# Attention stage: transposes of the outputs into the projection's PSUM tile, one projection product per unit by a table of steps, the final norm shared by ScalarE and VectorE

## The chip, the core and the metric

The kernel runs on one core of a Trainium2 chip. The metric is device time in microseconds (us) of one execution; the figure to beat is the median of three runs. A profile of one execution gives each engine's instructions: PE is TensorE's matmuls (PEld its weight loads), DVE is VectorE, ACT is ScalarE, POOL is GpSimd, SP is SyncE, which here only issues transfers (a q behind a name, as in SPq, means the engine's instruction queue).

## The reference, cut to what matters

The model has two layers; the change is in the second one, an attention over 2304 keys (256 of a context, 2048 of the sequence) for 2048 queries, 16 query heads that share 4 key heads, and in what follows it:

```
def attention_mixer(...):
    ...
    o_l = blocked_attention(q_l, k_all, v_all)      # softmax(q k / 8) v, head by head
    out_l = (o_l * jax.nn.silu(g_l)) @ w_out        # 2048 x 1024 by 1024 x 1024
    ...
def reference(...):
    ...
        h_lat = h_lat + gate[:, None] * o_lat
    return rms_norm(h_lat) * final_gain
```

`rms_norm` divides each row by the root of its mean square.

## The kernel before

`odd_attention` is the last stage of the program. The 2048 queries lie in 16 query tiles of 128 rows. A **unit** `u` is one query tile with one head, so there are 256 units, and 16 in a row make a query tile (`u // 16`). A loop runs over units and, inside a unit, over `b` = 0, 1, 2 (three thirds of the keys, 768 each). It is a hand-written software pipeline: in loop `u` the program works on four units at once, in this order:

- `s_step(u + 2, b)`: scores on PE into one of two PSUM buffers `s`, from which DVE copies them to `st` and takes their running maximum `mx` (line 1998);
- `split_step(u)` at b = 1: ACT makes the f16 high half `hi` of the transposed probabilities; `pv_end(u - 1)` at b = 2: ACT copies the result `r`;
- `exp_step(u + 1, b)`: ACT's exponential of `st` (line 2006), which needs the maximum over all three thirds; `n_step(u + 1, b)` at b = 0, 1: POOL splits probabilities into f16 halves `nat`;
- `t_step(u)` at b = 0: eight PE transposes of probabilities into the PSUM tile `tp` (line 2025), which has one buffer;
- `pv_step(u - 1)` at b = 0 and 1: 36 PE products with the values into `pv`;
- `d_step(u + 1, b)`: SP issues the transfer that transposes `nat` into `T`;
- `lower_step(u)` at b = 1: DVE makes the low half `lo` from `tp` (line 2035);
- then one entry of `small` (POOL's three steps on the outputs `o`) and one entry of the queue `todo[b]`.

When loop `w` = 16 (qt + 1) has ended a query tile, `finish` fills `todo[1]` and `todo[2]` with that tile's projection, and one entry of the queue of that `b` is taken per unit. Counting loops from `w`, the queues do this:

- loops w+1 and w+2, b = 2: `tr(0)` and `tr(1)`, four PE transposes of `o` each, **into a `tp` tile**, and from it ACT's `oh` (line 2102) and DVE's `ol` (line 35). `tr(0)` also loads the residual rows `h`;
- loops w+3 to w+13: the 16 products `mm` (three matmuls of 512 columns each, lines 2111 to 2113), three in two loops. `mm` 7 and 15 end an accumulation in the PSUM tile `po` (one buffer), and DVE adds it to `h` (line 2115);
- loop w+13: `norm`, ACT's square with a sum and two small POOL steps; w+14 and w+15, b = 1: `end(0)` and `end(1)`, one DVE instruction each (line 2122); w+16: the store.

So of the 16 loops between one `w` and the next, w+14, w+15 and w+16 have no product, w+1 and w+2 have the transposes. PSUM has eight banks; `s` takes four, `tp` two, `pv` and `po` one each.

Of the kernel before, what the change touches and what calls it, by code (L numbers as in the profile page):

```python
# [9 lines left out]
F32 = mybir.dt.float32  # L10
# [3 lines left out]
AF = mybir.ActivationFunctionType  # L14
ALU = mybir.AluOpType
# [4 lines left out]
P = 128  # L20
DM = 1024
KC = DM // P
T = 2304
NCTX = 256
# [9 lines left out]
def sub_lo(eng, lo, full, hi):  # L34
    eng.tensor_tensor(out=lo, in0=full, in1=hi.bitcast(F32), op=ALU.subtract)  # L35
# [10 lines left out]
def rms_rstd(E, pool, x, width, tag, junk):  # L46

    nc = E.nc
    ss = pool.tile([P, 1], F32, tag=tag + "s", name=tag + "s")
    nc.scalar.activation(out=junk, in_=x, func=AF.Square, accum_out=ss)  # L50
    r = pool.tile([P, 1], F32, tag=tag + "r", name=tag + "r")
    nc.gpsimd.tensor_scalar(out=r, in0=ss, scalar1=1.0 / width, scalar2=EPS, op0=ALU.mult, op1=ALU.add)
    nc.gpsimd.tensor_tensor(out=r, in0=r, in1=E.mhalf, op=ALU.pow)
    return r
# [1809 lines left out]
TCH = 8  # L1864
# [36 lines left out]
def odd_attention(E, out):  # L1901
    nc, I, S, tc = E.nc, E.I, E.S, E.tc
    v, gp = nc.vector, nc.gpsimd
    with ExitStack() as ctx:
        kp = ctx.enter_context(tc.tile_pool(name="at_k", bufs=2, side="right", reuse_waits="tile"))
        sp = ctx.enter_context(tc.tile_pool(name="at_l", bufs=2, reuse_waits="tile"))
# [3 lines left out]
        sps = ctx.enter_context(tc.tile_pool(name="at_s", bufs=1, space=PSUM, reuse_waits="tile"))  # L1910
        tps = ctx.enter_context(tc.tile_pool(name="at_t", bufs=1, space=PSUM, reuse_waits="tile"))
# [18 lines left out]
        fg = sp.tile([P, DM], F32, tag="fg", name="fg", bufs=1)  # L1930
# [44 lines left out]

        QT = [None] * 16
        UN = {}
        todo, small = ([], [], []), []

        def unit(u):  # L1980
            return u // 16, (u // 4) % 4, u % 4
# [22 lines left out]
        def exp_step(u, b):  # L2004
            st = UN[u]["st"][b]
            nc.scalar.activation(out=st, in_=st, func=AF.Exp, bias=UN[u]["mx"][:, 6:7])  # L2006
# [9 lines left out]
        def d_step(u, b):  # L2016
            T = UN[u]["T", b] = pp.tile([P, 2 * DCH[b], P], F16, tag=f"T{b}", name="T", bufs=2)
            nc.sync.dma_start_transpose(out=T, in_=UN[u]["nat", b].rearrange("p a c -> p (a c)"))
# [8 lines left out]
        def split_step(u):  # L2027
            hi, lo = [pp.tile([P, TCH, P], F16, tag=n, name=n, bufs=2) for n in ("hi", "lo")]
            pt = UN[u]["pt"]
            nc.scalar.activation(out=hi, in_=pt, func=AF.Copy)  # L2030
            UN[u]["hl"] = hi, lo
# [26 lines left out]
        def pv_end(u):  # L2058
            qt, kv, hh = unit(u)
            pv = UN[u]["pv"]  # L2060
            if u % 16 == 3:
                QT[qt] = sp.tile([P, DM], F32, tag="o", name="o", bufs=1)
            if u % 16 == 0:
                SG[qt] = sp.tile([P, DM], F32, tag="sg", name="sg", bufs=1)
                nc.sync.dma_start(out=SG[qt], in_=S["sg"][qt * P:(qt + 1) * P, :])
            if hh == 0:
                QR[kv % 2] = sp.tile([P, 4, 130], F32, tag="r", name="r")
            R = QR[kv % 2]
            nc.scalar.activation(out=R[:, hh, 0:129], in_=pv[:, 0:129], func=AF.Copy)
            if hh == 3:  # L2070
                oc = QT[qt][:, kv * 256:(kv + 1) * 256].rearrange("p (h d) -> p h d", d=HD)
                rs = sp.tile([P, 4, 1], F32, tag="rs", name="rs")
                v.reciprocal(rs, R[:, :, 64:65])
                of = QT[qt][:, kv * 256:(kv + 1) * 256]
                sgk = SG[qt][:, kv * 256:(kv + 1) * 256]
                small.extend([
                    lambda: gp.tensor_tensor(out=oc, in0=R[:, :, 0:64], in1=R[:, :, 65:129], op=ALU.add),
                    lambda: gp.tensor_tensor(out=oc, in0=oc, in1=rs.to_broadcast([P, 4, HD]), op=ALU.mult),
                    lambda: gp.tensor_tensor(out=of, in0=of, in1=sgk, op=ALU.mult)])
            del UN[u]  # L2080
            if u % 16 == 15:
                finish(qt)

        def finish(qt):

            qc = slice(qt * P, (qt + 1) * P)
            o = QT[qt]
            F = {}

            def tr(q):  # L2090
                if q == 0:
                    F["h"] = sp.tile([P, DM], F32, tag="h", name="h", bufs=1)
                    nc.sync.dma_start(out=F["h"], in_=S["h"][NCTX + qt * P:NCTX + (qt + 1) * P, :])
                    F["oh"] = sp.tile([P, KC, P], F32R, tag="oh", name="oh", bufs=1)
                    F["ol"] = sp.tile([P, KC, P], F32R, tag="ol", name="ol", bufs=1)
                pt = tps.tile([P, TCH, P], F32, tag="tp", name="tp")[:, :4].rearrange("p k t -> p (k t)")
                for k in range(4):
                    kk = 4 * q + k
                    nc.tensor.transpose(pt[:, k * P:(k + 1) * P], o[:, kk * P:(kk + 1) * P], E.ident)
                ks = slice(4 * q, 4 * q + 4)  # L2100
                p4 = pt.rearrange("p (k t) -> p k t", t=P)
                nc.scalar.activation(out=F["oh"][:, ks], in_=p4, func=AF.Copy)
                sub_lo(v, F["ol"][:, ks], p4, F["oh"][:, ks])

            def mm(c, k):
                cs = slice(c * 512, (c + 1) * 512)
                if k == 0:
                    F["po"] = sps.tile([P, 512], F32, tag="po", name="po", bufs=1)
                po, oh, ol = F["po"], F["oh"], F["ol"]
                wh, wl = W["wh"][:, k, cs], W["wl"][:, k, cs]  # L2110
                nc.tensor.matmul(po, oh[:, k], wh, start=(k == 0), stop=False)  # L2111
                nc.tensor.matmul(po, oh[:, k], wl, start=False, stop=False)  # L2112
                nc.tensor.matmul(po, ol[:, k], wh, start=False, stop=(k == KC - 1))  # L2113
                if k == KC - 1:
                    v.tensor_tensor(out=F["h"][:, cs], in0=po, in1=F["h"][:, cs], op=ALU.add)

            def norm():
                F["r"] = rms_rstd(E, sp, F["h"].rearrange("p (k c) -> p k c", c=P), DM, "fr", F["oh"])

            def end(c):  # L2120
                h, cs = F["h"], slice(c * 512, (c + 1) * 512)
                v.scalar_tensor_tensor(out=h[:, cs], in0=h[:, cs], scalar=F["r"], in1=fg[:, cs], op0=ALU.mult, op1=ALU.mult)

            def store():
                nc.sync.dma_start(out=out[qc, :], in_=F["h"])

            none = lambda: None
            products = [lambda c=c, k=k: mm(c, k) for c in range(2) for k in range(KC)]
            first = [none] * 2
            second = [none, lambda: tr(0), lambda: tr(1)]  # L2130
            while products:
                first.append(products.pop(0) if len(first) % 2 == 0 else none)
                if products:
                    second.append(products.pop(0))
            todo[1].extend(first + [lambda: end(0), lambda: end(1), store])
            todo[2].extend(second + [norm])

        NU = 256
        load_keys(0)
# [6 lines left out]
        for i in range(-2 * NTH, (NU + 2) * NTH):  # L2146
            u, b = divmod(i, NTH)
            if 0 <= i + VSTEP < NS // 3:
                values(i + VSTEP)
            out_weights(u, b)  # L2150
            live = lambda w: 0 <= w < NU
            if live(u + 2):
                s_step(u + 2, b)
            if b == 1 and live(u):
                split_step(u)
            if b == 2 and live(u - 1):
                pv_end(u - 1)
            if live(u + 1):
                exp_step(u + 1, b)
                if b < NTH - 1:  # L2160
                    n_step(u + 1, b)
            if b == 0 and live(u):
                t_step(u)
            if live(u - 1):
                for g in ((0,), (1, 2), ())[b]:
                    pv_step(u - 1, g)
            if live(u + 1) and b < NTH - 1:
                d_step(u + 1, b)
            if b == 1 and live(u):
                lower_step(u)  # L2170
            if small:
                small.pop(0)()
            if todo[b]:
                todo[b].pop(0)()
        while small:
            small.pop(0)()
        while todo[1] or todo[2]:
            for b in (1, 2):
                if todo[b]:
                    todo[b].pop(0)()  # L2180

# [151 lines left out]
```

## Time and profile before

| | |
|---|---|
| median of 3 runs | 4036.66 us (4035.59 to 4037.07) |
| profiled execution, its own time | 4034.8 us |
| its span, first to last instruction | 4033.1 us |
| attention loop in steady state | from about 2600 us to 4000 us |
| one query tile (16 units) in steady state | 92.19 us |

The profiled execution is 1.9 us below the median of the runs. A steady-state query tile repeats itself to within some hundredths of a us, so one of them, taken between the first probability transposes of loop w+1 (3182.16 us) and the same place 16 units later (3274.35 us), stands for all.

### The profile page before, as it was taken

How to read it: one execution, taken by the hardware profiler on the slowest of the kernel's cores; microseconds unless marked ns; L12 is line 12 of the kernel's file. 1: busy time of each engine (PE TensorE's matmuls, PEld its weight loads, DVE VectorE, ACT ScalarE, POOL GpSimd, SP SyncE). 2: the span in 40 equal slices, each digit the busy share in tenths (PEclk: the TensorE clock that was granted, in tenths of full speed). 3: DMA queues.
4: the chain of work that ended last, by engine and by line, in shares of the span. 5: the costliest groups of instructions: out<-in, count | busy, mean ns of one | idle time of the engine just before them, and what ended most of it. 6: DMA issues, size and time to landing. Idle time of an engine off the chain costs nothing.

```text
span 4033.1 us, 72188 instructions
## 1 busy us (share of the span) xinstructions
PE 3720.1 (92%) x27102; PEld 3145.1 (78%) x27102; DVE 2754.4 (68%) x5006; ACT 1850.9 (46%) x3195; POOL 2196.0 (54%) x2120
## 2 busy tenths in 40 slices
PE   7999998638889999999999997899999999999998
PEld 4888886316888888788778886788888888888887
DVE  5366767997687888711455453877777777777775
ACT  4422224203435565411222222666666666666665
POOL 2111113731233999522333332988888888888886
PEclk9999999869999999999999998999999999999999
DMA  7512323324667667533332225889888888888885
GB/s 262 176 56 66 98 69 93 109 66 118 210 221 257 228 235 241 191 123 131 129 110 85 94 79 146 173 143 159 162 157 154 154 153 157 152 151 158 153 163 115
DMA packets 998591, 594.49 MB, mean 147 GB/s; under 512 B 711849, under 2 KB 908249, under 8 KB 996193
## 3 DMA queue, kind: packets, MB, share of 16 engines
q1 hardware_dynamic: 984112, 563.35, 56.2%
q10 hardware_dynamic: 14128, 26.51, 1.8%
q8 instruction: 214, 3.51, 0.3%
q14 instruction: 137, 1.11, 0.1%
HBM read 296.63 MB, written 125.32 MB: 105 GB/s over the span
## 4 chain that ended last, share of the span: by engine, by line
PE 48%; DVE 5%; POOL 3%; issue 1%; DMA 1%; ACT 1%; SPq 0%; DVEq 0%; POOLq 0%; ACTq 0%
PE s L1996 11%; PE mm L43 6%; PE mm L41 6%; PE mm L42 6%; PE tp L2025 5%; PE pv L2054 5%; PE pv L2056 3%; PE po L2111 2%; DVE st L1998 2%; PE po L2112 1%; PE po L2113 1%; POOL nat L2014 1%; DVE lo L2035 1%; POOL nat L2013 1%; DVE ol L35 1%
## 5 line engine op out<-in xcount | busy, mean ns | idle before, releaser
L2006 ACT ACTIVATE st<-st,mx 128x768 f32<-128x768 f32 x768 | 714.5, 930 | 355.5 <-DVE mx L2002 271.8
L2014 POOL TENSOR_TENSOR nat<-st,nat 128x768 f16<-128x768 f32 (+1 forms) x512 | 727.0, 1420 | 42.7
L1996 PE MATMUL s<-KS,q 128*128 128x512 f32 (+1 forms) x3072 | 693.7, 351 | 40.3 <-DVE mx L1998 39.8
L1998 DVE CUSTOM_DVE_ANT_0 st<-s,zero,mx 128x768 f32<-128x768 f32 x512 | 519.3, 1014 | 278.8 <-PE s L1996 203.6
L1996 PEld LDWEIGHTS s<-KS,q 128*128 128x128 f32 x3072 | 536.1, 190 | 136.8 <-DVE mx L1998 47.7
L2013 POOL TENSOR_SCALAR nat<-st 128x768 f16<-128x768 f32 (+1 forms) x512 | 387.6, 757 | 187.4 <-ACT st L2006 187.2
L2025 PE MATMUL tp<-ident,st 128*128 128x128 f32 x2048 | 280.9, 277 | 36.4 <-DVE ol L35 22.3
L2035 DVE TENSOR_TENSOR lo<-tp,hi 128x1024 f16<-128x1024 f32 x256 | 312.3, 1220 | 2.9 <-ACT hi L2030 2.9
L2054 PE MATMUL pv<-V,T 128*128 128x129 f16 x2560 | 310.8, 222 | 2.4 <-DMA T<-nat 2.3
L41 PE MATMUL mmps<-ah,wh 128*128 128x512 f32 (+1 forms) x800 | 304.7, 381 | 3.8 <-DVE ah L214 3.8
L42 PE MATMUL mmps<-al,wh 128*128 128x512 f32 (+1 forms) x800 | 299.1, 374 | 0.3 <-DVE al L35 0.3
L43 PE MATMUL mmps<-ah,wl 128*128 128x512 f32 (+1 forms) x800 | 298.9, 374 | 0.0
L2030 ACT ACTIVATE hi<-tp 128x1024 f16<-128x1024 f32 x256 | 259.2, 1012 | 40.8 <-PE tp L2025 36.0
L2025 PEld LDWEIGHTS tp<-ident,st 128*128 128x128 f32 x2048 | 228.3, 142 | 62.5 <-DVE ol L35 28.4
L1998 DVE CUSTOM_DVE_ANT_0 st<-s,zero 128x768 f32<-128x768 f32 x256 | 243.0, 949 | 44.1 <-POOL nat L2014 26.1
L41 PE MATMUL mm<-w,ah 128*128 128x512 f32 x656 | 263.0, 401 | 1.5 <-ACT ah L1675 1.5
L42 PE MATMUL mm<-w,ah 128*128 128x512 f32 x656 | 257.2, 392 | 1.4 <-DVE w L35 1.4
L43 PE MATMUL mm<-w,al 128*128 128x512 f32 x656 | 257.5, 392 | 0.0
L2056 PE MATMUL pv<-V,T 128*128 128x65 f16 x2560 | 249.7, 193 | 0.0
L277 DVE SCALAR_TENSOR_TENSOR acc<-raw,convw,acc 128x512 f32<-128x512 f32 (+1 forms) x320 | 223.5, 698 | 35.8 <-POOL raw L270 11.8
L2054 PEld LDWEIGHTS <-T 128*128 128x128 f16 x2560 | 234.1, 97 | 14.2 <-DMA T<-nat 3.3
L2054 PE MATMUL pv<-V,hi 128*128 128x129 f16 x2048 | 220.7, 220 | 0.0
(429 smaller groups left out, 9094.4 us busy)
## 6 DMA issues: line engine op xcount, KB each, us to landing
ac<-acs SPq DMA_DIRECT2D x72, 512.0 KB
q<-q SPq DMA_DIRECT2D x128, 256.0 KB
x<-xn SPq DMA_DIRECT2D x35, 512.0 KB
h<-h SPq DMA_DIRECT2D x34, 512.0 KB
x<-in_x_dram SPq DMA_DIRECT2D x32, 512.0 KB
adaw<-in_ada_w_dram SPq DMA_DIRECT2D x32, 512.0 KB
a<-aT SPq DMA_DIRECT2D x32, 512.0 KB
wr<-in_ev_w_dram SPq DMA_DIRECT2D x38, 256.0 KB
```

The lines of the kernel that those rows point to most:

```text
L41: nc.tensor.matmul(ps, ah(k), bh(k), start=first and k == 0, stop=False)
L42: nc.tensor.matmul(ps, ah(k), bl(k), start=False, stop=False)
L43: nc.tensor.matmul(ps, al(k), bh(k), start=False, stop=last and k == n - 1)
L1996: nc.tensor.matmul(ps[:, c0:c0 + n], Q[:, hh % 2, i, hh // 2], KS[kv][:, b * TH + c0:b * TH + c0 + n], start=(i == 0), stop=(i == 1))
L1998: v.tensor_tensor_reduce(out=st, in0=ps[:, :TH], in1=zero.to_broadcast([P, TH]), scale=1.0, scalar=NEG if b == 0 else mx[:, b - 1:b], op0= ...
L2006: nc.scalar.activation(out=st, in_=st, func=AF.Exp, bias=UN[u]["mx"][:, 6:7])
L2013: gp.tensor_scalar(out=nat[:, 0], in0=p, scalar1=1.0, scalar2=0.0, op0=ALU.mult, op1=ALU.add)
L2014: gp.tensor_tensor(out=nat[:, 1], in0=p, in1=nat[:, 0], op=ALU.subtract)
L2025: nc.tensor.transpose(pt[:, j], UN[u]["st"][b][:, k * P:(k + 1) * P], E.ident)
L2035: v.tensor_tensor(out=lo, in0=UN[u]["pt"], in1=hi, op=ALU.subtract)
L2054: nc.tensor.matmul(pv[:, 0:129], hi, V2[:, c, kv, 0:129], start=first, stop=end)
L2056: nc.tensor.matmul(pv[:, 0:65], lo, V2[:, c, kv, 0:65], start=False, stop=False)
```

## The change

```
@@ finish
-                if q == 0:
-                    F["h"] = sp.tile([P, DM], F32, tag="h", name="h", bufs=1)
-                    nc.sync.dma_start(out=F["h"], in_=S["h"][NCTX + qt * P:NCTX + (qt + 1) * P, :])
...
-                pt = tps.tile([P, TCH, P], F32, tag="tp", name="tp")[:, :4].rearrange("p k t -> p (k t)")
+                pt = sps.tile([P, 512], F32, tag="po", name="pt", bufs=1)
...
@@ mm
+                if c == 0 and k == KC // 2:
+                    F["h"] = sp.tile([P, DM], F32, tag="h", name="h", bufs=1)
+                    nc.sync.dma_start(out=F["h"], in_=S["h"][NCTX + qt * P:NCTX + (qt + 1) * P, :])
@@ end
-                v.scalar_tensor_tensor(out=h[:, cs], in0=h[:, cs], scalar=F["r"], in1=fg[:, cs], op0=ALU.mult, op1=ALU.mult)
+                nc.scalar.activation(out=h[:, cs], in_=h[:, cs], func=AF.Copy, scale=F["r"])
+                v.tensor_tensor(out=h[:, cs], in0=h[:, cs], in1=fg[:, cs], op=ALU.mult)
@@ the table
-            todo[1].extend(first + [lambda: end(0), lambda: end(1), store])
-            todo[2].extend(second + [norm])
+            at = [(w + 1, 2), (w + 2, 2)] + [(w + j, 2) for j in range(3, 17)] + [(w + 6, 1), (w + 12, 1)]
+            at = sorted(at) + [(w + 17, 1), (w + 18, 1), (w + 19, 1), (w + 20, 1)]
+            for k, f in zip(at, [lambda: tr(0), lambda: tr(1)] + products + [norm, lambda: end(0), lambda: end(1), store]):
+                todo.setdefault(k, []).append(f)
@@ the loop
-            if todo[b]:
-                todo[b].pop(0)()
+            for f in todo.pop((u, b), []):
+                f()
```

The table keys each step by its loop and `b`. Loops w+3 to w+16 now have one product each, w+6 and w+12 two. `norm` moves to w+17, `end(0)` to w+18, `end(1)` to w+19, the store to w+20, which are loops w+1 to w+4 of the next query tile. The load of `h` moves from w+1 to the fifth product, loop w+6. The transposes stay where they were, but write the one-bank tile of `po`.

PE, first query tile, end of b = 1 and start of b = 2 in loop w+3; `s` are the scores, `pv` the products with the values, `po` a projection product. Lines with - are of before:

```order
 L2054 MATMUL pv<-V_21125,hi 128x129
-L2111 MATMUL po<-wh,oh 128x512
-L2112 MATMUL po<-wl,oh 128x512
-L2113 MATMUL po<-wh,ol 128x512
 L1996 MATMUL s<-KS_21120,q 128x512 x2
 L1996 MATMUL s<-KS_21120,q 128x256 x2
-L2111 MATMUL po<-wh,oh 128x512
-L2112 MATMUL po<-wl,oh 128x512
-L2113 MATMUL po<-wh,ol 128x512
+L2112 MATMUL po<-wh,oh 128x512
+L2113 MATMUL po<-wl,oh 128x512
+L2114 MATMUL po<-wh,ol 128x512
```

Of two products in this loop one is left; the other has moved to a later loop.

ACT around the norm. First before, loop w+13 and the one behind it (`st` exponentials, L50 the norm's square, `hi` and `r` as above):

```order
L2006 ACTIVATE st<-st,mx 128x768
L50 ACTIVATE oh,frs<-h 128x1024
L2006 ACTIVATE st<-st,mx 128x768
L2030 ACTIVATE hi<-tp 128x1024
L2006 ACTIVATE st<-st,mx 128x768
L2069 ACTIVATE r<-pv 128x129
L2006 ACTIVATE st<-st,mx 128x768
```

Then with the change, loops w+17 (from the square on) and w+18:

```order
L50 ACTIVATE oh,frs<-h 128x1024
L2069 ACTIVATE r<-pv 128x129
L2006 ACTIVATE st<-st,mx 128x768
L2100 ACTIVATE oh<-pt 128x512
L2006 ACTIVATE st<-st,mx 128x768
L2030 ACTIVATE hi<-tp 128x1024
L2006 ACTIVATE st<-st,mx 128x768
L2123 ACTIVATE h<-h,frr 128x512
L2069 ACTIVATE r<-pv 128x129
L2006 ACTIVATE st<-st,mx 128x768
L2100 ACTIVATE oh<-pt 128x512
```

The square now stands between a loop's second and third exponential, and so do the new copies that scale `h`; the copies `oh` of the next query tile stand in the same two loops.

DVE at the end of the program. Before, from the last `lo` but one:

```order
L2035 TENSOR_TENSOR lo<-tp,hi 128x1024
L2122 SCALAR_TENSOR_TENSOR h<-h,frr,fg 128x512
L2035 TENSOR_TENSOR lo<-tp,hi 128x1024
L2122 SCALAR_TENSOR_TENSOR h<-h,frr,fg 128x512
L2073 RECIPROCAL rs<-r 128x4
L35 TENSOR_TENSOR ol<-tp,oh 128x512 x2
L2115 TENSOR_TENSOR h<-po,h 128x512 x2
L2122 SCALAR_TENSOR_TENSOR h<-h,frr,fg 128x512 x2
```

And with the change:

```order
L2035 TENSOR_TENSOR lo<-tp,hi 128x1024 x2
L2073 RECIPROCAL rs<-r 128x4
L2116 TENSOR_TENSOR h<-po,h 128x512
L35 TENSOR_TENSOR ol<-pt,oh 128x512
L2124 TENSOR_TENSOR h<-h,fg 128x512
L35 TENSOR_TENSOR ol<-pt,oh 128x512
L2124 TENSOR_TENSOR h<-h,fg 128x512
L2116 TENSOR_TENSOR h<-po,h 128x512 x2
L2124 TENSOR_TENSOR h<-h,fg 128x512 x2
```

The last addition and the norm of the last query tile but one now come after the loop, between the steps of the last one.

## Rows read from the trace of the kernel before

**Rows 1.** The page's first part, busy time of each engine.

```profile
PE 3720.1 (92%) x27102; PEld 3145.1 (78%) x27102; DVE 2754.4 (68%) x5006; ACT 1850.9 (46%) x3195; POOL 2196.0 (54%) x2120
```

**Rows 2.** Windows of one query tile: transposes, products, rest; then their sum.

```profile
core 0: us, PE busy (x) PEld busy (x) DVE busy (x) ACT busy (x) POOL busy (x), PEclk, DMA share, GB/s
3182.16:3202.14 19.98, 17.28 (x183) 15.11 (x183) 14.82 (x30) 12.77 (x18) 16.61 (x18) 1.00 1.04 212
3202.14:3258.45 56.31, 56.31 (x605) 51.32 (x604) 42.59 (x84) 38.43 (x51) 46.11 (x47) 1.00 0.77 134
3258.45:3274.35 15.90, 15.15 (x170) 13.14 (x169) 14.81 (x27) 11.67 (x17) 14.15 (x15) 1.00 0.90 152
sum 92.19, PE 88.74 PEld 79.57 DVE 72.22 ACT 62.88 POOL 76.86; mean PE 29.58 PEld 26.52 DVE 24.07 ACT 20.96 POOL 25.62
```

**Rows 3.** Timeline of PE, same query tile: start, duration, instruction, [idle <- releaser].

```profile
3182.16 1.29 PE L2025 MATMUL tp<-ident,st 128*128 128x128 f32 x8
...
3187.15 0.63 PE L2099 MATMUL tp<-ident,o 128*128 128x128 f32 x4 [0.63 <-DVE lo L2035]
3187.54 0.93 PE L1996 MATMUL s<-KS,q 128*128 128x512 f32 x4
...
3189.20 1.09 PE L2025 MATMUL tp<-ident,st 128*128 128x128 f32 x8 [0.72 <-DVE ol L35]
...
3196.04 1.09 PE L2025 MATMUL tp<-ident,st 128*128 128x128 f32 x8 [0.72 <-DVE ol L35]
...
3202.14 1.04 PE L2025 MATMUL tp<-ident,st 128*128 128x128 f32 x8
...
3207.50 1.03 PE L2025 MATMUL tp<-ident,st 128*128 128x128 f32 x8
...
3213.56 1.03 PE L2025 MATMUL tp<-ident,st 128*128 128x128 f32 x8
...
3258.45 1.04 PE L2025 MATMUL tp<-ident,st 128*128 128x128 f32 x8
...
3268.97 1.29 PE L2025 MATMUL tp<-ident,st 128*128 128x128 f32 x8
...
3274.35 1.30 PE L2025 MATMUL tp<-ident,st 128*128 128x128 f32 x8
```

**Rows 4.** Waits, 2700 to 3900 us, 13 query tiles: us in total, times, longest.

```profile
PE tp L2025 <- DVE ol L35: 18.8, 26, 0.7
PE tp L2099 <- DVE lo L2035: 16.3, 26, 0.6
...
PE s L1996 <- DVE mx L1998: 6.4, 13, 0.5
```

**Rows 5.** Groups of instructions, 2700 to 3900 us: busy, mean ns, idle before.

```profile
L35 DVE TENSOR_TENSOR ol<-tp,oh 128x512 fp32r<-128x512 f32 x26 | 18.0, 692 | 8.3 <-ACT oh L2102 8.3
...
L2102 ACT ACTIVATE oh<-tp 128x512 fp32r<-128x512 f32 x26 | 15.6, 598 | 23.4 <-PE tp L2099 23.4
L50 ACT ACTIVATE oh<-h 128x1024 fp32r<-128x1024 f32 x13 | 13.8, 1060 | 9.4 <-DVE h L2115 9.4
```

**Rows 6.** The tile h, 2700 to 3900 us: ns min/median/max, first and last start.

```profile
L2115 DVE TENSOR_TENSOR h<-po,h x26: 678/686/693, 2704.3 to 3870.4; 128x512 f32<-128x512 f32 x26
L2122 DVE SCALAR_TENSOR_TENSOR h<-h,frr,fg x26: 745/1090/1358, 2709.8 to 3822.4; 128x512 f32<-128x512 f32 x26
```

**Rows 7.** Timeline of ACT, two loops: first and last of a loop's five steps.

```profile
3208.09 0.94 ACT L2006 ACTIVATE st<-st,mx 128x768 f32<-128x768 f32 x1 [1.43 <-DVE rs L2073]
...
3271.05 0.94 ACT L2006 ACTIVATE st<-st,mx 128x768 f32<-128x768 f32 x1 [1.72 <-DVE mx L2002]
...
3273.79 0.93 ACT L2006 ACTIVATE st<-st,mx 128x768 f32<-128x768 f32 x1
```

**Rows 8.** Timeline of SP at the end: last store but one, last load.

```profile
4005.14 0.57 SPq L2125 DMA_DIRECT2D out_dram<-h  x1
4008.18 0.33 SPq L2093 DMA_DIRECT2D h<-h  x1
```

More of the change, by code (lines that the diff above doesn't have):

```diff
@@ L1977, in odd_attention @@
         UN = {}
-        todo, small = ([], [], []), []
+        todo, small = {}, []
         def unit(u):
@@ L2081, in pv_end, with finish @@
             if u % 16 == 15:
-                finish(qt)
-        def finish(qt):
+                finish(qt, u + 1)
+        def finish(qt, w):
             qc = slice(qt * P, (qt + 1) * P)
@@ L2121, in end @@
                 h, cs = F["h"], slice(c * 512, (c + 1) * 512)
-                v.scalar_tensor_tensor(out=h[:, cs], in0=h[:, cs], scalar=F["r"], in1=fg[:, cs], op0=ALU.mult, op1=ALU.mult)
+                nc.scalar.activation(out=h[:, cs], in_=h[:, cs], func=AF.Copy, scale=F["r"])
+                v.tensor_tensor(out=h[:, cs], in0=h[:, cs], in1=fg[:, cs], op=ALU.mult)
             def store():
                 nc.sync.dma_start(out=out[qc, :], in_=F["h"])
-            none = lambda: None
             products = [lambda c=c, k=k: mm(c, k) for c in range(2) for k in range(KC)]
[L2129 to L2134, printed above, removed]
-            todo[1].extend(first + [lambda: end(0), lambda: end(1), store])
-            todo[2].extend(second + [norm])
+            at = [(w + 1, 2), (w + 2, 2)] + [(w + j, 2) for j in range(3, 17)] + [(w + 6, 1), (w + 12, 1)]
+            at = sorted(at) + [(w + 17, 1), (w + 18, 1), (w + 19, 1), (w + 20, 1)]
+            for k, f in zip(at, [lambda: tr(0), lambda: tr(1)] + products + [norm, lambda: end(0), lambda: end(1), store]):
+                todo.setdefault(k, []).append(f)
         NU = 256
@@ L2172, in odd_attention @@
                 small.pop(0)()
-            if todo[b]:
-                todo[b].pop(0)()
[L2175 to L2180, printed above, removed]
+            for f in todo.pop((u, b), []):
+                f()
+        for k in sorted(todo):
+            for f in todo[k]:
+                f()
 SCRATCH = {
```

## Prediction

> **What bounds the kernel now.** I read the page first, then windows over one query tile, then PE's timeline inside it, the waits, and last the durations of what is moved. The page says that PE is busy 92% of the span, ahead of every other engine [rows 1]. The windows say where it is not: over one query tile of 92.19 us, PE has no idle time in the ten loops w+4 to w+13 that hold 14 of the 16 products (56.31 of 56.31 us), and idles in the three loops before them (17.28 of 19.98) and the three behind (15.15 of 15.90) [rows 2]. So the middle is bound by PE's own work and the two ends by waits.
>
> PE's timeline gives the length of a loop, read from one first `tp` transpose to the next [rows 3]. A loop with one product takes 3207.50 - 3202.14 = 5.36 us, the next one, with two, 3213.56 - 3207.50 = 6.06. A product is therefore worth 0.70 and a loop without one 4.66. Check: ten loops and 14 products are 46.6 + 9.8 = 56.4, and 56.31 is there. Four transposes of `o` take 0.39 (3187.15 to the next scores at 3187.54), so a loop with them would take 5.05. With no waits the tile would cost:
> - w+1 to w+3 (two times four transposes, then two products): 5.05 + 5.05 + 6.06 = 16.2, against 19.98 measured: 3.8 lost;
> - w+4 to w+13: nothing lost;
> - w+14 to w+16: 3 x 4.66 = 14.0 against 15.90: 1.9 lost.
>
> That is 86.5 us of work and 5.7 us of waiting. The waits are named: the transposes of `o` wait for DVE's `lo` to free the one `tp` buffer, then the transposes of the probabilities wait in the same buffer for `ol`, 35.1 us in 13 tiles or 2.7 a tile [rows 4]; PE's weight loads, which stop too, make up the rest. In the loops without products, DVE's `end` steps (line 2122, 1.09 us at the median, up to 1.36 [rows 6]) hold up the maxima, and PE waits for a scores buffer (6.4 us in 13 tiles [rows 4]). Behind that ACT is late: its first exponential starts 2.08 after the loop's first transpose (3271.05 - 3268.97), where a one-product loop has 0.59 (3208.09 - 3207.50), and its five steps end at 3274.72, after PE has reached the next transposes at 3274.35; these then take 1.30 in place of 1.04 [rows 3, 7].
>
> **The change part by part.**
>
> *PE's work.* The same 8 transposes and 48 matmuls a tile are issued, only elsewhere: 12 loops with one product (5.36), two with two (6.06), two with transposes (5.05) make 64.3 + 12.1 + 10.1 = 86.5. The floor stays.
>
> *Transposes into `po`.* The 3.8 us go, since `lo`, `hi` and `tp` no longer meet them. What covers the new dependences: `tr(0)` needs the addition of product 15, one loop earlier, which ends some 2.7 us before it; `tr(1)` needs `oh` and `ol` of `tr(0)`, a loop earlier; product 0 needs those of `tr(1)`, with about 1.5 to spare. A longer lag of DVE would put it on PE one for one.
>
> *Products in every loop.* The 1.9 us go too, as the loops that were too short for ACT and DVE now have 0.70 more PE work. In a one-product loop ACT's five steps, 3.67 long when back to back (3271.05 to 3274.72 [rows 7]), are done 0.8 us or more before the next transposes need them.
>
> *The norm, now in loops that also have the transposes.* This is what costs. By rows, with `oh` 0.60, `ol` 0.69, the square 1.06 and its short read-out 0.19 at most [rows 5]:
> - w+17: the square delays the last exponential to 0.59 + 3.67 + 1.25 = 5.5; PE would take the next transposes at 5.05 and reach that exponential's part 0.2 later: 0.35 lost (estimate).
> - w+18: the copy of `end(0)` on ACT, DVE's multiplication ahead of the third maximum, `ol` behind it. The first exponential of w+19 starts at about 1.9 rather than 0.6.
> - w+19: with that lag and another copy the last exponential ends near 1.9 + 3.67 + 0.6 = 6.2, and scores wait for a buffer: 0.4 and 0.4 lost.
> - w+20: the lag is worked off with 0.25 lost; from w+21 on nothing.
>
> Sum 1.4 us a tile. ACT's new copy is not in the trace; its nearest row is `oh`, 512 columns, 0.60 [rows 5], and half of the square's 1024 gives 0.53, which changes nothing. DVE's new multiplication is not there either. Its lower bound is an instruction of that size with an operand in PSUM, 0.69 (`ol`, and the addition's 0.686); its upper one the old `end` at 1.36 [rows 5, 6]. With 0.69 the four loops lose only 0.6. I take 1.09, the median of the old `end`: it is nearest, because both read `h` and `fg` from SBUF while POOL works.
>
> So moving the scaling to ACT saves DVE nothing by my count: 1.09 before, 1.09 after. The Trainium skill, "SBUF — State Buffer", section "SBUF: two separate sides", says why that may be: a VectorE instruction with two SBUF inputs and a GpSimd instruction exclude each other from a port pair for a whole instruction, and dropping the scalar does not change the number of SBUF inputs. The trace agrees for the old step: 0.745 at the least, 1.358 at the most. By that page the four loops lose 1.4; were it a matter of the instruction's arithmetic, 0.6, and the forecast would be 12 us lower.
>
> *The load of `h`.* It leaves the moment at which `sg`, `h` and `q` are all issued (DMA share 1.04 in that window against 0.77 [rows 2]), and is issued at w+6 for use at w+9, some 16 us ahead; a store of the same size lands in about 3 us (4005.14 to 4008.18, when the load behind it could go [rows 8]). Its queue, SP, must first see the previous store land, issued 2.3 loops or 12 us earlier. Cost nothing; if the store were that late, SP's transfers `T` would stand behind it.
>
> *The end.* The last tile has no loops left, and the last but one now ends there too: product 15, its addition, the square, the scaling, and its store ahead of the last `h`. On that path 3 us of store and 3 us of load (bounded by the store) come before the last tile's first addition. I put it at 3.5 us later there, and 2.5 us won just before, where the norm no longer delays the last exponentials and products fill PE's wait. Net +1, between -1.5 and +4.
>
> **Sum.** A tile takes 86.5 + 1.4 = 87.9 in place of 92.2: 4.3 saved. Fifteen of the sixteen tiles run their projection inside the loop: 15 x 4.3 - 1 = 63 us. The profiled execution's 4034.8 (1.7 over its span) would become 3972; it lies 1.9 under the median of the runs, so 4036.7 - 63 = **3973.5 us** in the terms of the table.
>
> **Rivals.**
> - *The one-product loop is not sustained.* 5.36 was seen beside longer loops; 12 of 14 now have it. POOL has 4.61 us of work in such a loop (46.11 in ten), 86%, DVE 4.26, and the transfers' share would go from 0.77 to 0.81 [rows 2]. If the loops stay at today's mean of 5.63, 12 x 0.27 = 3.3 of the 4.3 are lost: 15 x 1.0 - 1 = 14 us saved, 4022. Against it: no engine is full, and PE had no wait there at all. Chance 0.14, spread between 3992 and 4022.
> - *The change doesn't do what it says:* the transposes wait as long in `po` as in `tp`, for an addition or an `ol` that is late. Then the 2.7 to 3.8 come back and 4.3 shrinks to about 1.1: 4021. Against it are the covers of 1.5 to 2.7 above. Chance 0.04.
> - *Slower:* ACT's copies need the norm's result from POOL, which queues behind the splits `nat` and the three output steps. I give it 0.85 us to spare in w+18. From there each us of POOL's lag stops ACT, with the exponentials queued behind the copy, and PE a loop later. It decides at 0.85 + 4.3 = 5.1 us of lag; with 6 us a tile loses 0.9 and the time is 4036.7 + 15 x 0.9 + 1 = 4051. POOL's 76.86 us in 88 (87%) speak for a lag, its 4.61 in 5.36 for one of 2 us at most. Chance 0.08.
> - *Nothing that can be told:* gains and new waits cancel, 4037. Chance 0.04.
>
> **How the numbers follow.** The forecast has 0.70: with the bounds of the multiplication (0.6 to 1.4 or a little more lost), of the end, and half a us a tile of error in my four loops it lies between 3952 and 3992. To leave out no more than 2 in 10 the range must reach into the first rival: 3952 to 4012. A difference of 0.2%, 8 us, is about what a measurement of this kernel can tell. Faster by more: 0.70 + 0.14 + 0.04 = 0.88; same 0.04; slower 0.08.
>
> **What would show it.** Tile length near 87.9; no waits of `tp` on `ol` or of the transposes of `o` on `lo`; loops w+4 to w+16 at 5.36 and 6.06 with PE full; DVE's multiplication near 1.1, not 0.7; short waits of PE in w+1 to w+4 on exponentials and maxima; the last store about 1 us later after the last loop. Wrong would be: PE idle in one-product loops (first rival), waits of the transposes on the addition or `ol` (second), ACT waiting for POOL's norm result (third).

## Result and the profile after

| | before | after |
|---|---|---|
| median, on the same chip | 4036.86 us (4035.59 to 4038.18, 4 runs) | 3976.21 us (3975.54 to 3977.15, 4 runs) |
| ratio | | 0.9848, interval 0.9833 to 0.9862 |
| profiled execution, and its span | 4034.8, 4033.1 | 3975.54, 3973.8 |
| one query tile in steady state | 92.2 us | 87.80 us |

The change saves 60.7 us, 1.5%. The forecast was 3973.5 with a tile of 87.9.

The page's first part and one window row of the changed kernel (columns as in [rows 1, 2]):

```profile
PE 3706.0 (93%) x27102; PEld 3147.9 (79%) x27102; DVE 2749.9 (69%) x5006; ACT 1859.6 (47%) x3227; POOL 2190.8 (55%) x2120
...
2700.00:3850.00 1150.00, 1144.10 (x12483) 1041.53 (x12482) 942.89 (x1807) 830.61 (x1128) 1005.15 (x1022) 1.00 0.92 163
```

The page hardly moves, because it is a mean over the whole program. The window over 13 query tiles shows the change: PE is busy in 1144.1 of 1150 us, 99.5%, where a tile of before had 88.74 of 92.19 [rows 2]. One tile, cut at loops w+1 to w+4 and w+5 to w+16:

```profile
3159.69:3181.93 22.24, 21.81 (x240) 19.53 (x239) 20.98 (x39) 17.88 (x26) 19.43 (x21) 1.00 0.88 167
3181.93:3247.49 65.56, 65.56 (x716) 59.96 (x715) 51.09 (x101) 45.51 (x60) 57.26 (x59) 1.00 0.94 162
sum 87.80, PE 87.37 PEld 79.49 DVE 72.07 ACT 63.40 POOL 76.69; mean PE 43.68 PEld 39.74 DVE 36.04 ACT 31.70 POOL 38.35
```

PE has no idle time in twelve of the sixteen loops, and the transfers' share is now 0.88 and 0.94 where it went from 1.04 to 0.77 and back to 0.90. PE's timeline gives the loops (first `tp` transposes, to set beside [rows 3]; transposes of `o` in the first two, two products in the loop that begins at 3187.29):

```profile
3159.69 1.04 PE L2025 MATMUL tp<-ident,st 128*128 128x128 f32 x8
...
3163.66 0.60 PE L2097 MATMUL pt<-ident,o 128*128 128x128 f32 x4
...
3164.81 1.13 PE L2025 MATMUL tp<-ident,st 128*128 128x128 f32 x8
...
3170.01 1.03 PE L2025 MATMUL tp<-ident,st 128*128 128x128 f32 x8
...
3176.09 1.29 PE L2025 MATMUL tp<-ident,st 128*128 128x128 f32 x8
...
3181.93 1.04 PE L2025 MATMUL tp<-ident,st 128*128 128x128 f32 x8
...
3187.29 1.03 PE L2025 MATMUL tp<-ident,st 128*128 128x128 f32 x8
...
3193.32 1.04 PE L2025 MATMUL tp<-ident,st 128*128 128x128 f32 x8
...
3198.67 1.04 PE L2025 MATMUL tp<-ident,st 128*128 128x128 f32 x8
```

The loops w+1 to w+4 last 5.12, 5.20, 6.08 and 5.84 us, then 5.36, 6.03, 5.35. Against 5.05, 5.05, 5.36 and 5.36 of work, the four lose 0.07, 0.15, 0.72 and 0.48: 1.4 in all. Only 0.43 of it is idle time of PE (22.24 less 21.81); the rest lies inside its records, as in the first transposes of w+4, which take 1.29 in place of 1.04. So 99.5% busy does not mean that nothing is left to win. Behind the transposes no wait on `ol` or `lo` is left. The waits of PE and PEld (2700 to 3850 us, 13 tiles: us in total, times, longest):

```profile
PEld s L1996 <- DVE mx L1998: 7.9, 15, 0.6
PE s L1996 <- DVE mx L1998: 5.6, 13, 0.4
...
PEld tp L2025 <- ACT st L2006: 2.8, 12, 0.2
```

So 35.1 us of waits in the `tp` buffer [rows 4] are gone, and what remains is a maximum that is late once a tile, and an exponential. The moved instructions (ns min/median/max), to set beside [rows 5, 6]:

```profile
L2116 DVE TENSOR_TENSOR h<-po,h x26: 660/678/692, 2721.2 to 3824.3; 128x512 f32<-128x512 f32 x26
L2123 ACT ACTIVATE h<-h,frr x26: 708/712/717, 2729.1 to 3789.3; 128x512 f32<-128x512 f32 x26
L2124 DVE TENSOR_TENSOR h<-h,fg x26: 681/1311/1600, 2730.4 to 3790.4; 128x512 f32<-128x512 f32 x26
```

**Where the time came from,** by the starts of `hi` (line 2030) in the two profiled executions: up to the loop's first `hi` 2499.6 and 2505.0 us, in code that the change does not touch (5.4 later); query tile 0, which has no projection beside it, 121.9 and 122.6 (0.7 longer); tile 1, 97.15 and 89.16 (8.0 saved); tiles 2 to 14, 92.21 and 87.80 on average (57.4 saved); the last 15 units 84.5 and 80.8 (3.7 saved); last `hi` to the end 31.15 and 34.78 (3.6 lost). The sum is 59.3, the difference of the spans. A second execution of each kernel (e11 and e12 below) gives, in the same order, 3.2 later, 2.5 longer, 6.0, 58.1 and 3.7 saved, and 2.9 lost: the steady tiles repeat, the other stretches move by 1 to 3 us.

### The profile page after: what moved, and what is told of

Read it like the earlier page. It is cut to its first block, busy times and chain, and to the rows that moved or that the text cites. A ratio compares the mean times of both kernels' runs of the same rounds, so it can differ in the third digit from the quotient of the medians.

```text
span 3973.8 us, 72150 instructions
## 1 busy us (share of the span) xinstructions
PE 3706.0 (93%) x27102; PEld 3147.9 (79%) x27102; DVE 2749.9 (69%) x5006; ACT 1859.6 (47%) x3227; POOL 2190.8 (55%) x2120
## 5 line engine op out<-in xcount | busy, mean ns | idle before, releaser
L1996 PE MATMUL s<-KS,q 128*128 128x512 f32 (+1 forms) x3072 | 708.5, 353 | 38.4 <-DVE mx L1998 38.4
```

The lines of the kernel that those rows point to most:

```text
L1996: nc.tensor.matmul(ps[:, c0:c0 + n], Q[:, hh % 2, i, hh // 2], KS[kv][:, b * TH + c0:b * TH + c0 + n], start=(i == 0), stop=(i == 1))
```

## Experiments

Ratios are to the kernel before on the same chip, with their intervals; tile lengths are the mean of tiles 2 to 14.

**e1: the changed kernel, transposes of `o` in a `tp` tile again.**

```
-                pt = sps.tile([P, 512], F32, tag="po", name="pt", bufs=1)
+                pt = tps.tile([P, TCH, P], F32, tag="tp", name="tp")[:, :4].rearrange("p k t -> p (k t)")
```

> The changed kernel with one part undone: the transposes of the outputs write a tp tile again; table of steps, split norm and late load stay. Theory (the move into po took away the waits of 3.8 us a query tile): the waits of the transposes on lo and of the next tp transposes on ol come back, a tile grows from 87.8 to about 91.2 us and the time from 3976 to about 4026. Rival (the table brings the gain, since it gives the short loops work): the time stays within 10 us of 3976.

4020.51 us (4011.74 to 4025.5), ratio 0.9956 (0.9939 to 0.9972); tile 90.25. The waits are back:

```profile
PE tp L2025 <- DVE ol L35: 22.0, 26, 0.9
PE tp L2097 <- DVE lo L2035: 16.2, 26, 0.6
```

The named waits, 38.2 us in 13 tiles or 2.9 a tile, are near the 2.7 of before, and the mechanism is shown. The tile grows by 2.45, less than expected. The loops w+1 to w+4 of one tile tell why:

```profile
3173.31 1.04 PE L2025 MATMUL tp<-ident,st 128*128 128x128 f32 x8
3180.16 1.09 PE L2025 MATMUL tp<-ident,st 128*128 128x128 f32 x8 [0.78 <-DVE ol L35]
3187.19 1.09 PE L2025 MATMUL tp<-ident,st 128*128 128x128 f32 x8 [0.91 <-DVE ol L35]
3192.61 1.04 PE L2025 MATMUL tp<-ident,st 128*128 128x128 f32 x8
3197.97 1.03 PE L2025 MATMUL tp<-ident,st 128*128 128x128 f32 x8
```

They last 6.85, 7.03, 5.42 and 5.36. Over 5.05, 5.05, 5.36 and 5.36 the first two lose 3.8, as before, but w+3 and w+4 lose almost nothing, where the changed kernel loses 1.2. DVE's multiplication takes 0.68 here, in place of 1.31 (last section), and a PE that stands in the buffer leaves ACT and DVE time for the norm; what each of the two gives was not tried. The profiled execution (4011.74) is the fastest of the four, 8.8 under their median, so the time misses the expected 4026 by less than the tile does.

**e2: the kernel before, with only the transposes in `po`.** The edit is the one above, the other way round.

> The kernel before with one part alone: the transposes of the outputs write the po tile; old queues, old end on DVE, old load of h. Theory: 3.3 to 3.8 of the 4.4 us a tile are already here, the 1.9 us of the loops without products stay: a tile of about 88.5 us, time 4037 - 15 x 3.6 = 3983, and the end of the program as before. Rival (without the table the loops behind the transposes are not ready to take the gain): at least 4010.

4018.97 us (4017.36 to 4023.43), ratio 0.9958 (0.9941 to 0.9975). The time is the rival's, and the tile only falls to 90.91, unevenly. Loops w+1 and w+2 shrink by 3.4 us, from 7.04 and 6.84 to 5.37 and 5.09, as the theory had it, but w+4 grows from 5.36 to between 6.25 and 9.79. Its waits, then SP's issues around such a loop, and a window in it:

```profile
POOL nat L2013 <- DMA T<-nat: 28.1, 12, 3.3
PEld L2054 <- DMA T<-nat: 26.4, 14, 3.0
PE pv L2054 <- DMA T<-nat: 23.0, 13, 2.7
```

```profile
3177.91 0.53 SPq L2125 DMA_DIRECT2D out_dram<-h  x1
3179.62 3.97 SPq L2018 DMA_TRANSPOSE T<-nat  x2
3183.64 0.57 SPq L2065 DMA_DIRECT2D sg<-sg  x1
3184.31 0.38 SPq L2093 DMA_DIRECT2D h<-h  x1
3184.74 1.25 SPq L1920 DMA_DIRECT2D q<-q  x2
3186.10 14.21 SPq L2018 DMA_TRANSPOSE T<-nat  x6
```

```profile
3190.00:3200.00 10.00, 7.36 (x62) 6.54 (x61) 4.66 (x9) 3.89 (x5) 6.18 (x7) 0.83 1.13 171
```

The store of the tile before goes out at 3177.91, and `sg`, `h` and both halves of `q` are issued one behind the other from 3183.64 to 3185.99, between the transfers that transpose `nat` into `T`. The DMA engines are full (share 1.13), `T` comes late, PE is busy in 7.36 of 10 us, and its granted clock falls to a mean of 0.83. SP is not held up by the store: the load of `h`, which has to follow it, goes out 0.10 behind `sg`. Before, PE stood waiting in the `tp` buffer in these loops, and from 2700 to 3900 us none of its waits is put down to `T`.

**e5: e2 with the late load of `h`** (at the fifth product, as in the change).

> The kernel before with two parts: transposes into po, and the load of h moved to the fifth product; old queues, old end. Theory (the move into po alone gained only 1.3 us a tile because store, sg, h and q then come close together and the transposed probabilities T come late in loop w+4): without h in that burst the waits for T shrink, a tile takes 88.3 to 89.3 us, time 3985 to 3998. Rival (the pace of three products in two loops is what holds the old queues, whatever is loaded when): the tile stays near 91 us, time 4010 or more.

3999.67 us (3998.26 to 4001.01), ratio 0.9911 (0.9894 to 0.9927); tile 89.35, both just above the theory's ranges and far from the rival's. The load's place is worth 19 us beside the transposes in `po`; PE's waits on `T` fall to

```profile
PE pv L2054 <- DMA T<-nat: 6.4, 8, 1.1
```

**e7: the changed kernel with `h` loaded early** (in `tr(0)`, with a second buffer, so that it need not wait for the store).

> The changed kernel with one part undone: h is loaded with the first transposes again, in loop w+1 with sg and q, for which its tile has two buffers. Theory (the late load keeps T in time): PE waits for T in loops w+2 to w+5, a tile of 88.3 to 90, time 3985 to 4010. Rival (with the products spread the burst does no harm, the load could be anywhere): 87.8 a tile, time 3974 to 3980.

3982.22 us (3979.33 to 3987.02), ratio 0.987 (0.9855 to 0.9884); tile 88.23. It lies between the two expectations: with the table the burst costs about 6 us, not 19 (6.0 by the medians; 6.5 by the tile, 15 times 0.43). The loss is in w+4, which takes up to 6.51 in place of 5.82. The two figures differ by more than the table: here `h` has a second buffer, and the store is issued behind the burst and not ahead of it. Which of these makes the burst cheaper was not tried. Its waits:

```profile
PEld L2054 <- DMA T<-nat: 8.5, 13, 1.0
PE pv L2054 <- DMA T<-nat: 5.4, 9, 0.7
```

**e3: the changed kernel with the old one-instruction end.**

```
-                nc.scalar.activation(out=h[:, cs], in_=h[:, cs], func=AF.Copy, scale=F["r"])
-                v.tensor_tensor(out=h[:, cs], in0=h[:, cs], in1=fg[:, cs], op=ALU.mult)
+                v.scalar_tensor_tensor(out=h[:, cs], in0=h[:, cs], scalar=F["r"], in1=fg[:, cs], op0=ALU.mult, op1=ALU.mult)
```

> The changed kernel with one part undone: the end of the norm is one DVE instruction again (h times r times gain), without ACT's copy. Theory (DVE's share got no shorter by the split, and ACT's copies of 0.71 us delay the exponentials): DVE's instruction takes 1.1 to 1.3 us as its successor does, a tile gets 0.2 to 0.5 us shorter, time 3968 to 3976. Rival (sharing helps DVE): DVE's instruction is longer than the multiplication, a tile grows, time 3980 or more.

3974.9 us (3971.32 to 3975.33), ratio 0.9843 (0.9829 to 0.9858); tile 87.85, and 33.35 from the last `hi` to the end in place of 34.78.

```profile
L2123 DVE SCALAR_TENSOR_TENSOR h<-h,frr,fg x26: 1095/1342/1599, 2730.1 to 3790.7; 128x512 f32<-128x512 f32 x26
```

In the same place the old instruction takes 1.34 and the new multiplication 1.31. The time is in the expected range, but the tile is not shorter by 0.2 to 0.5: the copies of ACT cost nothing in the loop, and sharing the norm gains nothing there. Of the 1.4 us behind the loop 0.6 are the copy's: from the last product to the end of the span it is 8.07 here and 8.65 with the change. The other 0.8 lie ahead of it, mostly in products that run for longer at a low granted clock, which differs between executions of one kernel too (below).

**e4 and e6: the ends in quarters.** e4 cuts `end` into four pieces of 256 columns in w+19 to w+22, stores in w+23 and loads `h` two products later:

```
+                if c == 0 and k == KC - 2:
...
+                h, cs = F["h"], slice(c * 256, (c + 1) * 256)
...
+            at = sorted(at) + [(w + j, 1) for j in (17, 19, 20, 21, 22, 23)]
```

> The changed kernel with the end of the norm in four quarters of 256 columns in loops w+19 to w+22 (none in the loops with transposes), store at w+23, load of h at the seventh product. Theory (the 1.3 us that are left over the work of 86.5 come from DVE falling behind where transposes and ends meet): the waits of PE on maxima and exponentials go, a tile takes 86.6 to 86.9, time about 3962. Rival (the rest is not DVE's lag but POOL's or the transfers' at a one-product pace): a tile stays at 87.5 or more, time 3973 or more.

3967.95 us (3962.36 to 3969.97), ratio 0.9826 (0.9811 to 0.984); tile 87.14, uneven (86.6 to 88.0): between the two expectations. PE's waits on the maxima are gone, 0.5 us in 13 tiles. In their place `h` comes late for its addition, and now and then `T`:

```profile
DVE h L2116 <- DMA h<-h: 7.5, 8, 1.6
...
PE pv L2054 <- DMA T<-nat: 3.2, 6, 1.0
```

e6 is e4 with the one-instruction end and `sg` loaded two loops later (`u % 16 == 2`).

> The quarter ends with two more edits: each quarter is one DVE instruction without ACT's copy, and sg is loaded two loops later, at w+3, apart from q. Theory (what the quarter ends left over 86.5 us are waits for T behind the burst of sg and q): no waits for T, a tile of 86.6 in every query tile, time about 3962. Rival: the tiles stay uneven between 86.6 and 88, time 3966 to 3970.

3961.68 us (3957.66 to 3966.35), ratio 0.9818 (0.9803 to 0.9833); tile 86.87. The time is as expected and no wait on `T` is left. The tile is not: 86.6 was expected of every one, and they run from 86.62 to 87.62, because the wait on `h` stays: where they lose, it is in loop w+10 (up to 6.30 us), behind the addition that waits.

**e8, e9, e10: halves, moved behind the transposes.** e8 keeps the two one-instruction ends, but in w+19 and w+20, with the store in w+21, `h` loaded at the sixth product and `sg` two loops later:

```
-            if u % 16 == 0:
+            if u % 16 == 2:
...
-                if c == 0 and k == KC // 2:
+                if c == 0 and k == KC - 3:
...
-            at = sorted(at) + [(w + 17, 1), (w + 18, 1), (w + 19, 1), (w + 20, 1)]
+            at = sorted(at) + [(w + j, 1) for j in (17, 19, 20, 21)]
```

> The changed kernel with the two ends as one DVE instruction each in loops w+19 and w+20, away from the transposes, store at w+21, h loaded at the sixth product and sg two loops later. Theory (the place of the ends, not their number, makes the waits of w+2 to w+4): 86.7 to 87.0 a tile, time 3962 to 3966. Rival (an end of 1.3 us is too long for a one-product loop wherever it stands): 87.4 or more, time 3971 or more.

**3955.12 us** (3952.09 to 3957.68), ratio 0.9801 (0.9786 to 0.9816), the lowest median of all and below the expected range. The tile is 86.64, and PE is never idle in the window:

```profile
2700.00:3850.00 1150.00, 1149.97 (x12633) 1053.96 (x12632) 944.62 (x1833) 828.19 (x1117) 1018.59 (x1036) 1.00 0.92 165
```

e9 is the changed kernel with the late `sg` alone, e10 is e8 with `sg` at its old place.

> The changed kernel with one edit: the load of sg is issued two loops later (u % 16 == 2 in place of 0). Theory: what the changed kernel still loses in loops w+3 and w+4 (6.08 and 5.82 us against 5.35) is the norm's steps meeting the transposes of o on ACT and DVE; the load of sg has no part in it. Then the tile stays at 87.8 us and the time within 3971 to 3978 us. Rival: the load of sg, issued beside q at the beginning of a query tile, delays transfers that PE needs there; then the tile goes to 86.6 to 87.2 us and the time to 3956 to 3967.

3971.35 us (3970.34 to 3974.21), ratio 0.9836 (0.9819 to 0.9852); tile 87.81, the four loops as with the change: the place of `sg` gives nothing there.

> The changed kernel with the old one-instruction end in loops w+19 and w+20, the store in w+21 and the load of h one product later (the sixth); sg is loaded where the changed kernel loads it. Theory: with the ends one and two loops behind the transposes of o, loops w+3 and w+4 go to 5.36 us, the tile to 86.6 to 86.8 and the time to 3954 to 3961 us. Rival: the later load of sg was needed for it, as without it a transfer T comes late now and then; then the tile is uneven, 87.0 to 87.4, and the time 3962 to 3970 us.

3963.91 us (3958.46 to 3968.78), ratio 0.9818 (0.9803 to 0.9832); tile 86.97, uneven (86.3 to 87.5): the rival, whose 87.0 to 87.4 are just missed. The ends' place gives 0.8 us a tile, with `h` loaded one product later, which was not tried by itself; only then does the place of `sg` count, with 0.3 more, since `T` is late without it:

```profile
PEld L2054 <- DMA T<-nat: 4.8, 10, 0.8
PE pv L2054 <- DMA T<-nat: 2.4, 7, 0.6
```

**e11 and e12: both kernels once more,** for the moment at which the loop begins.

> The kernel before once more, for the place in time at which the attention loop begins (the first hi). It stood at 2499.6 us before and at 2505.0 with the change, in code that the change does not touch. Theory: it varies from execution to execution; then it may stand anywhere between 2498 and 2507 us here. Rival: it belongs to the program; then it stands at 2499.6 within 1 us. The tile must be at 92.2 us again.

> The changed kernel once more, for the same place. Theory (it varies): anywhere between 2498 and 2507 us. Rival (it belongs to the program): 2505.0 within 1 us. The tile must be at 87.8 us again.

Before began at 2503.5 us (2499.6 the first time) and took 4038.57; the changed kernel began at 2506.7 (2505.0) and took 3979.31. The tiles were 92.27 and 87.80. So the moment varies by some us within a kernel. From it to the end of the span before took 1533.5 and 1533.3 us, the changed kernel 1468.8 and 1470.9 (the first execution of each named first): the change saves 62 to 65 us where it acts. That the changed kernel also begins later on average is neither shown nor excluded by two executions of each.

## Why the prediction was right, step by step

- *The work of a tile, 86.5.* Right. e8 comes to 86.64 with PE never idle: the floor is real, and the change stays 1.2 above it.
- *The waits in the `tp` buffer go.* Right as a mechanism and in size: with the buffer back, w+1 and w+2 lose 3.8 again (e1). None came in their place in `po` (second rival): inside the loop the transposes of `o` wait neither for the addition nor for `ol`.
- *One-product loops keep their 5.36.* Right: 5.35 in all of them from w+5 on, with PE full. The first rival is out, and it had most of the chance against the forecast. The 1.9 of the loops without products are gone with it.
- *1.4 lost in w+1 to w+4.* The sum is right, 1.4, in part by luck, for its parts miss in both directions. They were put at 0.35, 0, 0.8 and 0.25 and measured 0.07, 0.15, 0.72 and 0.48. The multiplication takes 1.31 in place of 1.09 (1.59 in w+2 and 1.04 in w+3), ACT's copy 0.71 in place of 0.60. The price of 1.09 was a median over other places: each such instruction of DVE ends some 0.55 after the instruction of POOL that was running when it began, so its time follows from where it stands (last section). The lag in w+3 is the one foreseen: the first exponential starts at 3172.17, 2.16 after the loop's first transpose (1.9 was expected).
- *Moving the scaling to ACT saves DVE nothing.* Right, and e3 shows it: 1.31 against 1.34. At the end of the program, where POOL stands idle, the multiplication takes 0.69, so it is not its arithmetic.
- *ACT waits for POOL's norm* (the slower rival). In the loop no such wait occurs; at the end of the program there are two, 1.3 us together.
- *The load of `h` costs nothing.* Its size was right, the account was not. I saw the burst (share 1.04 [rows 2]), and counted the load's new place as free and without gain. Left early, the load costs 19 us where the transposes are in `po` without the table (e2 against e5) and about 6 in the changed kernel (e7): the waits that the edit removes had covered transfers that would come late, and I did not ask what PE would meet when it came there sooner.
- *The end, +1.* Mis-sized: 3.6 later behind the last `hi` (2.9 in the second executions). I counted the stores and loads of `h` there, but no engine is seen to wait for a load of `h`. On the path, however, is the one `po` buffer, through which the two transposes, the additions and the first product now go one after another. PE's timeline at the end (start, duration, instruction, idle before it), first before, then with the change, and windows of the changed kernel there:

```profile
4010.25 0.41 PE L2099 MATMUL tp<-ident,o 128*128 128x128 f32 x2 [1.56 <-DVE ol L35]
...
4011.03 0.48 PE L2111 MATMUL po<-wh,oh 128*128 128x512 f32 x1
```

```profile
3945.73 0.63 PE L2097 MATMUL pt<-ident,o 128*128 128x128 f32 x4 [0.88 <-DVE h L2116]
...
3948.27 0.74 PE L2097 MATMUL pt<-ident,o 128*128 128x128 f32 x4 [1.91 <-DVE ol L35]
...
3950.42 0.79 PE L2112 MATMUL po<-wh,oh 128*128 128x512 f32 x1 [1.41 <-DVE ol L35]
```

```profile
3945.70:3950.40 4.70, 1.36 (x8) 0.83 (x8) 2.11 (x4) 3.59 (x6) 1.59 (x4) 0.81 0.01 3
3950.40:3955.60 5.20, 5.18 (x13) 4.09 (x13) 0.57 (x1) 0.00 (x0) 0.00 (x0) 0.51 0.38 124
```

  Counted from the last `hi`, the first product of the last tile starts at 11.4 us (3950.42 less 3939.01); before it was 9.1 (4011.03 less 4001.93). That is 2.3 of the 3.6, and 1.9 in the second executions. In the 4.7 us ahead of that product PE is busy for 1.36 only; after them the granted clock stands at 0.51, which is the 1.2 GHz level, and the first products take 0.63 where later ones take 0.39. Before showed the same, but for fewer products (mean 0.70 from 4010 to 4015 us). The eight products of the first half take 0.75 longer for it, and 0.41 in the second executions. The remaining 0.6 lies behind the last product and is ACT's copy: from that product to the end of the span the changed kernel takes 8.65 and 8.66, while e3, which lacks only the copy, takes 8.07, and so do before, e2, e5 and e8 with the same one-instruction end, to 0.01.
- *The sum.* 15 tiles x 4.3 was 64.5, and 69.1 came: fourteen stretches gave 4.4 or a little less each, but tile 1 gave 8.0, because before took 5 us longer there (97.15) than in steady state. Against it stand the end, 3.6 lost in place of 1, and 6.1 in the start and tile 0, for which the sum had no term: 69.1 - 3.6 - 6.1 = 59.4. That the whole came so near to the forecast of 63 (60.7 by the medians) is luck in part: the three parts miss by +4.6, -2.6 and -6.1.

## What to carry to other kernels

A wait that is removed must be followed to what PE would meet next. Here the buffer wait hid transfers that would come late, and neither that edit alone (17 us) nor the rest without it (18 us) gives a third of what the whole gives (61 us). When the engine that bounds is at 99.5%, the remaining loss is found by asking which loops have work of two kinds on the same engines: moving the norm's last two steps behind the transposes, with the old end, and loads to a quieter place, gave about 20 us more without taking an instruction from PE (e8). And the program's last tile pays alone for a buffer that the loop hides.

## What the runs showed of the hardware

**A VectorE instruction with both inputs in SBUF and a GpSimd instruction that reads SBUF hold each other up.** In the changed kernel DVE's multiplication meets POOL's splits; DVE's row, then POOL's (start, duration):

```profile
3169.42 1.59 DVE L2124 TENSOR_TENSOR h<-h,fg 128x512 f32<-128x512 f32 x1
```

```profile
3168.80 1.67 POOL L2014 TENSOR_TENSOR nat<-st,nat 128x768 f16<-128x768 f32 x1
3170.42 1.07 POOL L2013 TENSOR_SCALAR nat<-st 128x512 f16<-128x512 f32 x1
```

The multiplication starts while POOL's instruction runs, and ends 0.54 after that one's end (3171.01 against 3170.47). POOL's next one, 0.65 on average, then takes 1.07. All 26 multiplications from 2700 to 3850 us end 0.54 to 0.56 after the POOL instruction in which they began, and so do all 26 old ends of the kernel before from 2700 to 3900 us. With POOL idle, at the end of the program, the multiplication takes 0.69. In e1 the same multiplication starts together with POOL's instruction:

```profile
2733.47 0.68 DVE L2124 TENSOR_TENSOR h<-h,fg 128x512 f32<-128x512 f32 x1
```

```profile
2733.47 1.71 POOL L2014 TENSOR_TENSOR nat<-st,nat 128x512 f16<-128x512 f32 x1
```

Here the two starts agree to the hundredth, DVE needs 0.68 (679/682/915 ns over 26), and POOL pays: 1.71, where this form takes 1.19 on average in the changed kernel. The Trainium skill, "SBUF — State Buffer", section "SBUF: two separate sides", says that of a VectorE instruction with two SBUF inputs and a GpSimd one that reads SBUF, whichever starts first has the shared ports for the whole instruction and the other blocks. The trace agrees, with 1.59 us on the one side and 1.71 on the other, except that the wait is some 0.15 shorter than a whole instruction: 0.54 where the multiplication alone takes 0.69. Which of the two came first where both start at 2733.47 the trace cannot tell.

**Parts of a change need not add up.** By their ratios, times 4037 us, the transposes in `po` give 17 us (e2), with the late load 36 (e5), with the table and the shared norm 61; the table and the late load without `po` give 18 (e1). The late load is worth 19 us beside the transposes alone and about 6 in the whole change (e7, by medians and tiles).

**Where a kernel's code is unchanged, its start still moves:** the first `hi` of the attention loop stood between 2498.3 and 2507.2 us over twelve kernels and two repeats, on several chips. What makes it do so was not tried.
